# First input tiles given out by two DMA queues in one-tile pieces, first weight heads split on VectorE, seven warm-up matmuls for nine

## The chip, the cores and the metric

The kernel runs on one core of one Trainium2 chip. The metric is the time of one execution in microseconds; three runs of the kernel before and one profiled execution are at hand. TensorE is PE in the profile, VectorE DVE, ScalarE ACT, GpSimd POOL; SP is the engine that only issues DMAs, and ACT and POOL can issue them too.

## What is computed

One layer of a hybrid decoder over 512 tokens of width 1024, all in f32. Only the start matters here: the first of the projections, of which the change touches three output tiles.

```
h = rms_norm(x, norm_mix)            # x: (512, 1024)
z = h @ w_in
... z_mq ... = split(z)              # z_mq: the queries of the memory cross-attention
```

After it come the other mixers, the output projection, a gated MLP with a short convolution, and a last norm.

## The kernel before

x lies transposed in eight tiles of 128 channels by 512 tokens (`xs["T"][k]`, m in the profile's names, k = 0 to 7). The first three query tiles (u = 0 to 2) are made by `start`: for each k and each u, a weight tile of 128x128 times x tile k, summed over k in three PSUM banks. For precision every f32 operand is split in two parts of the type f32r, a rounded one (hi) and the rest (lo), and three matmuls stand for one: hi x hi, hi x lo, lo x hi. So a k has 9 matmuls, and `start` has 72. RMSNorm's gain is put on x in the split of x (`x_split`: ACT makes hi at L371, DVE makes lo at L372); the row scale comes later.

`split` makes a weight's parts: ACT copies to hi (L97), DVE subtracts to lo (L98). In `start` the raw weights of unit u come in pieces of two k (128x256, 128 KB), between the x tiles (256 KB each), all on the SP queue. The gain column needed by `x_split` is in `prm`, whose first eight columns are a DMA of their own (L200), the first on the SP queue. The rest of `prm` is the seventh DMA there (L426).

Ahead of that, PE multiplies a tile of zeros (`warm`) NWARM = 9 times (L211) and ACT loads its function table with an Exp of one column (L208). The order on each engine is set by a scheduler from the order of the code and its own estimate of times, so an edit here can also move instructions later on. After `start` come three more query tiles (`qu`), x's mean square (L219 to L228), the scale broadcast (L237, L238), the eight normalized tiles (`x_norm`, L392) and the keys and values of the memory.

Of the kernel before, what the change touches and what calls it, by code (L numbers as in the profile page):

```python
# [8 lines left out]
F32 = mybir.dt.float32  # L9
# [4 lines left out]
AF = mybir.ActivationFunctionType  # L14
ALU = mybir.AluOpType
# [3 lines left out]
P = 128  # L19
D = 1024  # L20
KD = D // P
# [19 lines left out]
BRANCHES = (2, 0, 1)  # L41
NRAW = 3
HT = S // 2
NWARM = 9


C_GMIX = 0
# [10 lines left out]
def trunk(ctx: ExitStack, tc: tile.TileContext, x, xT, mem, memT, par, wdecay, wch, wv, wg, wmk,  # L58
          wmv, wrg, wbr, wout, wup, wdown, wdown2, gffn, gfin, out):
    nc = tc.nc  # L60
# [11 lines left out]
    def nm(s):  # L72
        uid[0] += 1
        return f"{s}_{uid[0]}"
# [4 lines left out]
    def rslot(shape=(P, S)):  # L79
        return apool.tile(list(shape), F32R, tag="s", name=nm("r"))  # L80

    def mslot(dt=F32, shape=(P, S)):
        return hpool.tile(list(shape), dt, tag="m", name=nm("m"), bufs=8)

    def bank(shape=(P, S)):
        return psm.tile(list(shape), F32, tag="mm", name=nm("mm"))

    def sbank(shape=(P, S)):
        return pss.tile(list(shape), F32, tag="sm", name=nm("sm"))

    def stat(n, p=P):
        return small.tile([p, n], F32, tag=f"st{n}", name=nm("st"), bufs=12)


    def split(hi, lo, src, eng=None):

        nc.scalar.activation(hi, src, AF.Copy)  # L97
        return (eng or nc.vector).tensor_tensor(out=lo, in0=src, in1=hi.bitcast(F32), op=ALU.subtract)  # L98
# [98 lines left out]

    HB = D // 2
    prm = const.tile([P, NPAR], F32, name="prm")
    nc.sync.dma_start(prm[:, :KD], par[:, :KD])  # L200
    ident = const.tile([P, P], F32, name="ident")
    make_identity(nc, ident)
    ones = const.tile([P, P], F32, name="ones")
# [1 line left out]

    warm = const.tile([P, P], F32, name="warm")
    nc.vector.memset(warm, 0.0)
    nc.scalar.activation(stat(1), warm[:, 0:1], AF.Exp)  # L208
    ps = sbank((P, P))
    for _ in range(NWARM):  # L210
        nc.tensor.matmul(ps, lhsT=warm, rhs=warm, start=True, stop=True)  # L211

    def col(c, p=P):
        return prm[:p, c:c + 1]
# [151 lines left out]
    xs = {"T": [mslot() for _ in range(KD)], "r": []}  # L366

    def x_split(ks):
        for k in ks:
            r, g, src = (rslot(), rslot()), col(C_GMIX + k), xs["T"][k]  # L370
            nc.scalar.activation(r[0], src, AF.Copy, scale=g)  # L371
            nc.vector.scalar_tensor_tensor(out=r[1], in0=src, scalar=g, in1=r[0].bitcast(F32),  # L372
                                           op0=ALU.mult, op1=ALU.subtract)
            xs["r"].append(r)

    def x_squares(ks):
        for k in ks:
            xs["acc"] = add_square(xs.get("acc"), xs["T"][k])
# [19 lines left out]
    def queries(ps):  # L398
        r = (rslot(), rslot())
        if len(mq) % 3 == 1:  # L400
            for q, own, other in zip(r, (slice(0, 64), slice(64, P)), (slice(64, P), slice(0, 64))):
                nc.scalar.activation(q[own], ps[own], AF.Copy)
                nc.vector.tensor_tensor(out=q[other], in0=ps[own], in1=q[own].bitcast(F32), op=ALU.subtract)
        else:
            split(*r, ps)
        mq.append(r)

    def start():


        n = 3
        raw = [wpool.tile([P, D], F32, tag="raw", name=nm("raw"), bufs=NRAW) for _ in range(n)]
        whi, wlo = ([[wpool.tile([P, D], F32R, tag=t, name=nm(t))] for _ in range(2)] + [[rslot(), rslot()]]
                    for t in ("whi", "wlo"))

        def w(a, u, k, m=1):
            j, k = divmod(k, KD // len(a[u]))
            return a[u][j][:, k * P:(k + m) * P]

        for k in range(0, KD, 2):  # L420
            nc.sync.dma_start(xs["T"][k], xT[:, k, :])
            for u in range(n):
                nc.sync.dma_start(raw[u][:, k * P:(k + 2) * P], wch[u][:, k * P:(k + 2) * P])
            nc.sync.dma_start(xs["T"][k + 1], xT[:, k + 1, :])
            if k == 0:
                nc.sync.dma_start(prm[:, KD:], par[:, KD:])  # L426
        for k in range(0, KD, 2):
            x_split([k])
            for u in range(n):
                split(w(whi, u, k, 2), w(wlo, u, k, 2), raw[u][:, k * P:(k + 2) * P])  # L430
            x_split([k + 1])
        ps = [bank() for _ in range(n)]
        for k in range(KD):
            seq = [(whi, u, j) for j in range(2) for u in range(n)] + [(wlo, u, 0) for u in range(n)]
            for i, (a, u, j) in enumerate(seq):
                nc.tensor.matmul(ps[u], lhsT=w(a, u, k), rhs=xs["r"][k][j], start=k == 0 and i < n,  # L436
                                 stop=k == KD - 1 and i >= len(seq) - n)
        x_squares(range(4))
        for p in ps:
            queries(p)  # L440

    step(start)
    qu = [(wch[i], D, lambda w: queries(channel_major(w, KD, lambda k: xs["r"][k]))) for i in range(3, NM)]
    xn = [lambda k=k: x_norm(k) for k in range(KD)]
# [1073 lines left out]
```

## Time and profile before

| | |
|---|---|
| median of three runs | 923.41 us (923.1 to 926.32) |
| profiled execution, its own time | 924.37 us |
| profiled execution, span from first to last instruction | 922.6 us |
| mean granted TensorE clock | 0.997 |
| PE busy | 912.0 us, 99% of the span |

The span is the stretch of the recorded instructions; the execution's own time holds 1.77 us more around it. PE's busy time is the time in which a matmul was under way, waiting inside a matmul's record included.

### The profile page before, as it was taken

The numbers are of one execution on the slowest core, as the hardware profiler recorded it, in microseconds if no ns is written. First come the engines' busy times: TensorE is split into PE (matmuls) and PEld (weight loads), VectorE is DVE, ScalarE is ACT, GpSimd is POOL, SyncE is SP. The second block draws the span as 40 slices with busy tenths as digits, with TensorE's granted clock in tenths as the row PEclk, the third lists the DMA queues.
The fourth block names the chain that finished last, engine by engine and source line by source line (L and its number), as shares of the span: only waits on it lengthen the run. The fifth ranks groups of instructions, "written<-read, shape, count | busy, mean of one in ns | idle before, by whom it ended". The sixth has DMA issues, their size and how long they took to land.

```text
span 922.6 us, 12732 instructions
## 1 busy us (share of the span) xinstructions
PE 912.0 (99%) x4606; PEld 784.1 (85%) x4606; DVE 657.2 (71%) x1168; ACT 524.1 (57%) x888; POOL 128.1 (14%) x168
## 2 busy tenths in 40 slices
PE   9999999999999999999999999999999999999997
PEld 7899888888889998888888898998988888888885
DVE  6997755665689568746766678767787757598765
ACT  7765655685865468474534446555555445445544
POOL 0010000000243430320000000222111130013102
PEclk9999999999999999999999999999999999999998
DMA  7446223213467884321157313675646785357622
GB/s 238 148 137 214 92 88 101 88 42 119 110 170 167 187 204 126 115 86 53 52 157 258 116 59 90 157 185 130 148 114 165 145 228 125 114 137 181 139 69 91
DMA packets 51183, 123.27 MB, mean 134 GB/s; under 512 B 6145, under 2 KB 14001, under 8 KB 51121
## 3 DMA queue, kind: packets, MB, share of 16 engines
q1 hardware_dynamic: 35648, 94.99, 31.6%
q0 software_dynamic: 15328, 27.21, 17.3%
q8 instruction: 36, 0.59, 0.3%
q10 hardware_dynamic: 144, 0.26, 0.1%
q14 instruction: 27, 0.21, 0.1%
HBM read 117.99 MB, written 3.67 MB: 132 GB/s over the span
## 4 chain that ended last, share of the span: by engine, by line
PE 87%; DMA 5%; DVE 3%; issue 2%; ACT 2%; POOL 0%; SPq 0%; DVEq 0%; POOLq 0%; ACTq 0%
PE mm L104 78%; DMA f<-in_wup 4%; PE sm L104 3%; DMA f<-in_wv 2%; PE mm L436 2%; DVE wlo L98 1%; DVE r L98 1%; ACT r L97 1%; PE sm L211 0%; PE sm L996 0%; PE sm L983 0%; PE sm L1010 0%; DVE f L810 0%; PE sm L1147 0%; PE sm L601 0%
## 5 line engine op out<-in xcount | busy, mean ns | idle before, releaser
L97 ACT ACTIVATE whi<-raw 128x1024 fp32r<-128x1024 f32 (+3 forms) x142 | 135.5, 961 | 144.4 <-PE mm L104 113.1
L98 DVE TENSOR_TENSOR wlo<-raw,whi 128x1024 fp32r<-128x1024 f32 (+3 forms) x142 | 157.4, 1113 | 82.8 <-ACT whi L97 39.4
L104 PE MATMUL mm<-whi,r 128*128 128x512 f32 (+2 forms) x568 | 171.2, 372 | 0.0
L104 PEld LDWEIGHTS mm<-whi,r 128*128 128x128 f32 x568 | 105.5, 188 | 15.9 <-ACT r L97 0.3
L104 PE MATMUL mm<-hh,whi 128*128 128x512 f32 x288 | 113.4, 394 | 0.0
L104 PE MATMUL mm<-hl,whi 128*128 128x512 f32 x288 | 112.8, 392 | 0.0
L104 PE MATMUL mm<-wlo,r 128*128 128x512 f32 (+2 forms) x284 | 105.7, 372 | 0.5 <-DVE wlo L98 0.5
L104 PE MATMUL mm<-h2l,whi 128*128 128x512 f32 x264 | 102.8, 390 | 0.0
L104 PE MATMUL mm<-h2h,whi 128*128 128x512 f32 x264 | 102.7, 390 | 0.0
L98 DVE TENSOR_TENSOR r<-f,r 128x512 fp32r<-128x512 f32 (+3 forms) x144 | 79.7, 577 | 23.0 <-ACT r L97 22.7
L104 PE MATMUL mm<-r,whi 128*128 128x512 f32 (+1 forms) x432 | 94.2, 367 | 0.0
L97 ACT ACTIVATE r<-f 128x512 fp32r<-128x512 f32 (+3 forms) x144 | 70.1, 535 | 34.1 <-DMA f<-in_wup 29.2
L98 DVE TENSOR_TENSOR wlo<-f,whi 128x512 fp32r<-128x512 f32 (+2 forms) x90 | 53.8, 631 | 47.5 <-ACT whi L97 40.6
L104 PEld LDWEIGHTS mm<-r,whi 128*128 128x128 f32 x432 | 75.2, 189 | 13.1
L97 ACT ACTIVATE whi<-f 128x512 fp32r<-128x512 f32 (+2 forms) x90 | 48.2, 579 | 62.5 <-PE mm L104 48.8
L104 PE MATMUL mm<-hh,wlo 128*128 128x512 f32 x288 | 71.4, 390 | 0.0
L104 PE MATMUL mm<-r,r 128*128 128x512 f32 (+2 forms) x336 | 65.7, 346 | 0.3 <-ACT r L97 0.3
L104 PE MATMUL mm<-h2h,wlo 128*128 128x512 f32 x264 | 65.2, 389 | 0.0
L104 PEld LDWEIGHTS mm<-hh,wlo 128*128 128x128 f32 x288 | 54.0, 188 | 11.2
L104 PEld LDWEIGHTS mm<-hh,whi 128*128 128x128 f32 x288 | 54.1, 188 | 10.8
L104 PEld LDWEIGHTS mm<-hl,whi 128*128 128x128 f32 x288 | 54.1, 188 | 10.7
L104 PEld LDWEIGHTS mm<-r,r 128*128 128x128 f32 (+1 forms) x336 | 53.3, 186 | 9.6 <-ACT r L97 0.5
(261 smaller groups left out, 1545.2 us busy)
## 6 DMA issues: line engine op xcount, KB each, us to landing
raw<-in_wch SPq DMA_DIRECT2D x39, 512.0 KB, 3.3
raw<-in_wup SPq DMA_DIRECT2D x36, 512.0 KB, 4.0
f<-in_wdown POOLq DMA_DIRECT2D x40, 256.0 KB, 7.0
raw<-in_wbr SPq DMA_DIRECT2D x24, 384.0 KB, 3.1
raw<-in_wdown SPq DMA_DIRECT2D x14, 512.0 KB, 3.8
f<-in_wup SPq DMA_DIRECT2D x24, 256.0 KB, 6.9
f<-in_wup POOLq DMA_DIRECT2D x24, 256.0 KB, 6.4
f<-in_wdown SPq DMA_DIRECT2D x20, 256.0 KB, 4.7
```

The source lines that it names most:

```text
L97: nc.scalar.activation(hi, src, AF.Copy)
L98: return (eng or nc.vector).tensor_tensor(out=lo, in0=src, in1=hi.bitcast(F32), op=ALU.subtract)
L104: nc.tensor.matmul(ps, lhsT=l, rhs=r, start=first and i == 0, stop=last and i == len(seq) - 1, skip_group_check=more)
L436: nc.tensor.matmul(ps[u], lhsT=w(a, u, k), rhs=xs["r"][k][j], start=k == 0 and i < n, stop=k == KD - 1 and i >= len(seq) - n)
```

## The change

The first k gets pieces of its own. Its three weight heads (columns 0 to 127 of each unit) and the small `prm` piece are issued on the ACT queue; x tiles 0 and 1 and the second heads (columns 128 to 255) on the SP queue; the large `prm` piece on the POOL queue. The table load with its Exp now stands behind ACT's four DMA issues. The first heads' hi and lo are both made on DVE (a copy, then a subtraction); x tile 0 is split after them, and the second heads after the hi part of x tile 0. Pieces from k = 2 on are as before. Two warm-up matmuls are left out.

```diff
-NWARM = 9
+NWARM = 7
...
-    nc.sync.dma_start(prm[:, :KD], par[:, :KD])
+    nc.scalar.dma_start(prm[:, :KD], par[:, :KD])
...
-    nc.scalar.activation(stat(1), warm[:, 0:1], AF.Exp)
...
-            nc.scalar.activation(r[0], src, AF.Copy, scale=g)
+            xs["head"] = nc.scalar.activation(r[0], src, AF.Copy, scale=g)
...
-        for k in range(0, KD, 2):
+
+        nc.sync.dma_start(xs["T"][0], xT[:, 0, :])
+        for u in range(n):
+            nc.scalar.dma_start(raw[u][:, :P], wch[u][:, :P])
+        nc.scalar.activation(stat(1), warm[:, 0:1], AF.Exp)
+        nc.sync.dma_start(xs["T"][1], xT[:, 1, :])
+        for u in range(n):
+            nc.sync.dma_start(raw[u][:, P:2 * P], wch[u][:, P:2 * P])
+        nc.gpsimd.dma_start(prm[:, KD:], par[:, KD:])
+        for k in range(2, KD, 2):
             nc.sync.dma_start(xs["T"][k], xT[:, k, :])
...
-            if k == 0:
-                nc.sync.dma_start(prm[:, KD:], par[:, KD:])
-        for k in range(0, KD, 2):
+        for u in range(n):
+            nc.vector.tensor_copy(w(whi, u, 0), raw[u][:, :P])
+            nc.vector.tensor_tensor(out=w(wlo, u, 0), in0=raw[u][:, :P], in1=w(whi, u, 0).bitcast(F32), op=ALU.subtract)
+        x_split([0])
+        with tc.issue_after(xs["head"].ins):
+            x_split([1])
+        with tc.issue_after(xs["head"].ins):
+            for u in range(n):
+                split(w(whi, u, 1), w(wlo, u, 1), raw[u][:, P:2 * P])
+        for k in range(2, KD, 2):
             x_split([k])
```

On ACT, at the program's start, this stood before (m is an x tile, raw a weight piece, whi and the r made from raw are weight hi parts):

```order
L208 ACT_TABLE_LOAD
L208 ACTIVATE st_87<-warm 128x1
L371 ACTIVATE r_158<-m_101,prm 128x512
L97 ACTIVATE whi_129<-raw_126 128x256
L97 ACTIVATE whi_130<-raw_127 128x256
L97 ACTIVATE r_131<-raw_128 128x256
L371 ACTIVATE r_168<-m_102,prm 128x512
```

and this stands there now, with every line number behind the edit moved on by up to 15:

```order
L200 DMA prm<-in_par 128x8
L422 DMA raw_122<-in_wch 128x128
L422 DMA raw_123<-in_wch 128x128
L422 DMA raw_124<-in_wch 128x128
L423 ACT_TABLE_LOAD
L423 ACTIVATE st_137<-warm 128x1
L370 ACTIVATE r_165<-m_97,prm 128x512
L370 ACTIVATE r_169<-m_98,prm 128x512
L97 ACTIVATE whi_125<-raw_122 128x128
L97 ACTIVATE whi_126<-raw_123 128x128
L97 ACTIVATE r_127<-raw_124 128x128
```

Four DMA issues came ahead of the table load, and the three weight copies between x tile 0 and x tile 1 went away.

On DVE, right behind the zeroing of `warm`, this stood before:

```order
L372 SCALAR_TENSOR_TENSOR r_159<-m_101,prm,r_158 128x512
L98 TENSOR_TENSOR wlo_133<-raw_126,whi_129 128x256
L98 TENSOR_TENSOR wlo_134<-raw_127,whi_130 128x256
L98 TENSOR_TENSOR r_135<-raw_128,r_131 128x256
L372 SCALAR_TENSOR_TENSOR r_169<-m_102,prm,r_168 128x512
```

and this stands there now:

```order
L434 CAST whi_125<-raw_122 128x128
L435 TENSOR_TENSOR wlo_129<-raw_122,whi_125 128x128
L434 CAST whi_126<-raw_123 128x128
L435 TENSOR_TENSOR wlo_130<-raw_123,whi_126 128x128
L434 CAST r_127<-raw_124 128x128
L435 TENSOR_TENSOR r_131<-raw_124,r_127 128x128
L371 SCALAR_TENSOR_TENSOR r_166<-m_97,prm,r_165 128x512
L371 SCALAR_TENSOR_TENSOR r_170<-m_98,prm,r_169 128x512
```

Six instructions of 128x128 came ahead of the lo part of x tile 0 (r_166 now, r_159 before).

On PE the first k's nine matmuls stood like this before (r_158 and r_159 are hi and lo of x tile 0):

```order
L211 MATMUL sm_89<-warm 128x128 x9
L436 MATMUL mm_214<-r_158,whi_129 128x512
L436 MATMUL mm_215<-r_158,whi_130 128x512
L436 MATMUL mm_214<-r_159,whi_129 128x512
L436 MATMUL mm_215<-r_159,whi_130 128x512
L436 MATMUL mm_216<-r_158,r_131 128x512
L436 MATMUL mm_216<-r_159,r_131 128x512
L436 MATMUL mm_214<-r_158,wlo_133 128x512
```

and now (r_165 and r_166 are hi and lo of x tile 0):

```order
L210 MATMUL sm_87<-warm 128x128 x7
L451 MATMUL mm_221<-r_165,whi_125 128x512
L451 MATMUL mm_222<-r_165,whi_126 128x512
L451 MATMUL mm_223<-r_165,r_127 128x512
L451 MATMUL mm_221<-r_166,whi_125 128x512
L451 MATMUL mm_222<-r_166,whi_126 128x512
L451 MATMUL mm_223<-r_166,r_127 128x512
L451 MATMUL mm_221<-r_165,wlo_129 128x512
```

The third unit's hi matmul moved up to third place, ahead of the three with x's lo part. Behind `start` the same instructions stand on PE, DVE and ACT, some of them a few rows earlier or later, up to about the 465th row of PE's list; from there on the lists agree. SP issues two DMAs fewer, those of `prm`, ahead of x tile 2.

## Rows read from the trace of the kernel before

**Rows 1.** Page: the span; PE's busy time, share and instructions.
```profile
span 922.6 us, 12732 instructions
PE 912.0 (99%) x4606; PEld 784.1 (85%) x4606; DVE 657.2 (71%) x1168; ACT 524.1 (57%) x888; POOL 128.1 (14%) x168
```

**Rows 2.** Timeline of PE, 0 to 26 us: start, us, operation, idle before.
```profile
1.13 4.21 PE L211 MATMUL sm<-warm 128*128 128x128 f32 x18 [1.13 <-DVE warm L207]
5.26 1.90 PE L436 MATMUL mm<-r,whi 128*128 128x512 f32 x4
7.00 0.63 PE L436 MATMUL mm<-r,r 128*128 128x512 f32 x2
...
8.16 0.63 PE L436 MATMUL mm<-r,whi 128*128 128x512 f32 x2
...
22.46 3.79 PE L104 MATMUL mm<-r,whi 128*128 128x512 f32 x16
```

**Rows 3.** Timeline of PE, 24 to 140 us: the rows with idle time before.
```profile
67.85 0.44 PE L104 MATMUL mm<-wlo,r 128*128 128x384 f32 x1 [0.49 <-DVE wlo L98]
105.15 0.55 PE L620 MATMUL sm<-ident,f 128*128 128x128 f32 x3 [0.26 <-ACT f L607]
```

**Rows 4.** Timeline of ACT, 0 to 9 us.
```profile
0.81 1.28 ACT L208 ACT_TABLE_LOAD   x1 [0.81 <-PEq L1507]
2.10 0.20 ACT L208 ACTIVATE st<-warm 128x1 f32<-128x1 f32 x1
4.18 0.72 ACT L371 ACTIVATE r<-m,prm 128x512 fp32r<-128x512 f32 x1 [1.87 <-DMA m<-in_xT]
4.80 0.40 ACT L97 ACTIVATE whi<-raw 128x256 fp32r<-128x256 f32 x1
...
7.07 0.73 ACT L371 ACTIVATE r<-m,prm 128x512 fp32r<-128x512 f32 x1 [0.30 <-DMA m<-in_xT]
```

**Rows 5.** Chain of work, 0 to 130 us: start, us, what.
```profile
5.34 17.28 PE mm L436 x72
...
41.69 0.22 PE sm L238 x2
```

**Rows 6.** Timeline of PE's weight loads around 6.3 us.
```profile
6.15 0.34 PEld L436 LDWEIGHTS mm<-r,whi 128*128 128x128 f32 x1
6.54 0.19 PEld L436 LDWEIGHTS mm<-r,whi 128*128 128x128 f32 x1
```

**Rows 7.** Timeline of SP's DMA issues, 0 to 9 us.
```profile
0.81 0.39 SPq L200 DMA_DIRECT2D prm<-in_par  x1
1.26 0.43 SPq L421 DMA_DIRECT2D m<-in_xT  x1
1.74 1.37 SPq L423 DMA_DIRECT2D raw<-in_wch  x3
```

**Rows 8.** Timeline near the end: the one DMA issue on ACT's queue.
```profile
918.96 0.37 ACTq L1390 DMA_DIRECT2D out<-f  x1
```

**Rows 9.** Landing of x 0, weight pieces 0 and 2, x 1 (us from issue).
```profile
m<-in_xT SPq DMA_DIRECT2D x1, 256.0 KB, 2.8
raw<-in_wch SPq DMA_DIRECT2D x1, 128.0 KB, 2.7
raw<-in_wch SPq DMA_DIRECT2D x1, 128.0 KB, 3.6
m<-in_xT SPq DMA_DIRECT2D x1, 256.0 KB, 3.9
```

**Rows 10.** Line L237, DVE on 128x128: duration in ns, min/median/max.
```profile
L237 DVE TENSOR_SCALAR dg<-ident,st x6: 278/282/334, 40.9 to 53.3; 128x128 f32<-128x128 f32 x6
```

**Rows 11.** Timeline of DVE, 0 to 9 us.
```profile
4.93 0.75 DVE L372 SCALAR_TENSOR_TENSOR r<-m,prm,r 128x512 fp32r<-128x512 f32 x1 [3.86 <-ACT r L371]
5.60 0.79 DVE L98 TENSOR_TENSOR wlo<-raw,whi 128x256 fp32r<-128x256 f32 x2
```

**Rows 12.** Windows, DVE alone: stretch, us, busy (instructions), clock, DMA, GB/s.
```profile
50.00:54.00 4.00, 4.00 (x11) 1.00 0.28 94
```

## The prediction

> **What bounds the kernel now.** I read the page first. PE is busy 912.0 of 922.6 us [rows 1], so only what keeps PE from its next matmul can pay, and the whole idle time is 10.6 us. Then PE's timeline [rows 2]: the warm-ups run from 1.13 to 5.34, the first matmul of `start` begins at 5.26, the second k at 8.16, and `start` is done at 22.46, when the next unit follows without a gap. From 8.16 to 22.46 lie 63 matmuls, k = 1 to 7, so one takes 14.30 / 63 = 0.227 us and PE never waits in that stretch. The first k's nine matmuls would need 9 x 0.227 = 2.04 us and take 8.16 - 5.26 = 2.90. This is the only place that the change can shorten directly, together with the 5.26 us ahead of it. From 24 to 140 us PE stands idle in two places only, 0.49 and 0.26 us [rows 3]. So an earlier end of `start` moves all later work on PE, as long as those two waits don't grow.
>
> Why the first k is slow: its hi matmul waited for the weight's hi part, which ACT made from 4.80 to 5.20, after x tile 0's hi part from 4.18 to 4.90 [rows 4]; ACT itself had waited 1.87 us for x tile 0. And PE runs at its lower level there. A warm-up pass of 128 columns takes 4.21 / 18 = 0.234 us, while the like pass at L238 takes 0.22 / 2 = 0.11 [rows 2, 5]: 1.2 against 2.4 GHz. The weight load at 6.15 still takes 0.34 us, the one at 6.54 takes 0.19 [rows 6], so the clock rises between them, near 6.4, after PE has worked without a long pause since 1.13. (The column of the granted clock shows 1.00 throughout, so durations are my guide.) A matmul of 512 columns costs about 2 x 0.227 = 0.45 us before that moment.
>
> **The change part by part.**
>
> *ACT's queue and x tile 0.* SP's issues start 0.45 to 0.48 us apart [rows 7]; the only issue on ACT's queue takes 0.37 [rows 8]. Four of them ahead of the table load take 4 x 0.37 = 1.5 to 4 x 0.46 = 1.84 us; I take the upper value, since those of SP are at the same place in the program. ACT gets to the table load at 0.81 + 1.84 = 2.65, ends it at 3.93 and the Exp at 4.13 [rows 4]. x tile 0 is now issued at 0.81 and not at 1.26, and with 2.8 us to landing [rows 9] it is there at about 3.6. So its split begins at about 4.15 (lower bound 3.85, by the shorter issues), against 4.18: this part gains nothing, since ACT takes the place of the DMA as the last to come. Hi of x tile 0 is ready at 4.15 + 0.72 = 4.87.
>
> The table load stands right before the Exp [rows 4]: 1.28 us, and the Exp starts 0.01 us later. The Trainium skill (ScalarE: Activation LUTs, What ACT_TABLE_LOAD costs) adds a drain of about 1.38 us to the load of 1.28, some 2.66 together. By the page the split of x would begin at about 5.5, by the row at 4.15: the trace agrees with the load's length and shows no drain behind it, and what stands behind four DMA issues no row shows.
>
> *The weight heads on DVE.* They are issued at about 1.27, 1.73 and 2.19, each 64 KB. Of the 128 KB pieces the first took 2.7 us to land, the third 3.6 [rows 9], behind x tile 0 in one queue. I take 2.7 for all, as half the bytes: 4.0, 4.45, 4.9; upper bound for the third, with 3.6, 5.8. A DVE instruction of 128x128 takes 0.28 us [rows 10], so a head's copy and subtraction take 0.57. The first hi part is there at 4.3, before x's hi part. So the first matmul begins at 4.87 + 0.03 = 4.9, against 5.26. The last pair ends at 4.9 + 0.57 = 5.5 (upper bound 6.4). DVE's lo part of x tile 0 is queued behind it, where before it was DVE's first work at 4.93 [rows 11]: now 5.5 to 6.25 (upper bound 7.15).
>
> *PE.* Three hi matmuls at 0.45 each run 4.9, 5.35, 5.8, to 6.25; the third head's hi part (5.2) is in time. The next six, which need x's lo part, can go at 6.3. If the clock rises near 6.4 as before, they take 6 x 0.227 = 1.36 us and the first is a little slower: the second k begins at 7.7, against 8.16. **Gain: 0.45 us.** With the upper bound of the landings the lo part is there at 7.15 and the second k begins at 8.55, a loss of 0.4; with the lower bound of ACT's issues the three hi matmuls are over by 6.0, DVE still sets 6.25, and the gain stays at about 0.5.
>
> *The warm-ups.* Seven end at 1.13 + 14 x 0.234 = 4.41, so two fewer never hold up the first matmul; PE then idles 0.5 us. That costs nothing unless the clock answers to it (first rival).
>
> *The later tiles.* x tile 1, issued at 1.27, lands with at most 3.9 us [rows 9] at 5.2 (before: 7.07 [rows 4]); ACT makes its hi part until 5.9, then three heads of 128x128; DVE makes its lo part until 7.0 and three heads at 0.28 until 7.85, needed at 7.7 + 6 x 0.227 = 9.1. No wait. SP has two `prm` issues fewer ahead of x tile 2, so that is no later than before, and from there on PE had the data in time without a gap. The large `prm` piece goes through POOL, free by then; it is read first by a small ACT instruction at about 12 us. Nothing.
>
> *The reordered instructions and the wait at 67.85.* PE's place is given to it by DVE there [rows 3], and DVE is busy without a pause in 50 to 54 us [rows 12]. If DVE doesn't come earlier by as much, part of the 0.45 goes into that wait. DVE's work is released by PE's own results from further back (the mean square and broadcast matmuls), so most should move along; I take 0.05 off.
>
> Sum: 0.45 - 0.05 = 0.4. The profiled execution's own 924.37 becomes 923.97; it lies 0.96 above the median of 923.41, and against that median I forecast **923.0 us**, 0.04% less. A measurement of this kernel can tell about 0.5% (4.6 us) from no change, more than `start`'s whole lead of 5.26 us is likely to give.
>
> **Rivals.**
>
> *The clock rises later* (slower). PE has less work before 6.4: warm-ups until 4.41, an idle half microsecond, three matmuls. The Trainium skill (TensorE: Matmul & The Clock Gate, What's actually happening) says that the low clock is the default and that activity releases it, which speaks against taking warm-ups out; the rows above agree that the first 5 us run at the low level. No row gives a later moment for the rise; as a bound I let it come with the third k of the old order, at 10.2: until then PE does (10.2 - 4.9) / 0.45 = 11.8 matmuls, where before 9 + (10.2 - 8.16) / 0.227 = 18 were done. The loss is 6.2 x 0.227 = 1.4 us, so **924.8**. It decides from a rise later than about 7.3: each 0.45 us more at the low level costs one matmul's 0.227, so 0.9 us of it cost the whole gain. For it speaks the gap; against it that PE also had a gap before, inside the 1.90 us of the first four matmuls.
>
> *ACT or the heads are late* (a new wait). A pause on ACT as long as the table load itself, 1.28, would make x's hi part ready at 6.15 and begin the second k at about 6.3 + 2.04 = 8.35, a loss of 0.2; the upper landing bound gave a loss of 0.4. With 0.3 this is **923.7**. For it speaks that four issues are put ahead of the table load; against it that the row shows the load followed by the Exp at once. The drain in the Trainium skill (ScalarE: Activation LUTs, What ACT_TABLE_LOAD costs) would be such a pause.
>
> *The gain is eaten at 67.85.* The wait grows from 0.49 to 0.9 and **923.4** stays.
>
> *More than forecast.* The clock rises when it did or earlier, the lo part is ready at 6.0, and one of the two later waits vanishes by the new order: 0.45 + 0.25 + 0.49 = 1.2, so **922.2**.
>
> **How the numbers follow.** Forecast 0.40, late clock 0.20, late ACT or heads 0.15, eaten 0.13, more 0.10, something unseen 0.02. The range reaches from the "more" case to the late clock, with the spread of the shown executions around their median (0.3 below, 1 above) taken in half: 921.9 to 925.0. No case comes near 4.6 us: faster 0.01, same 0.97, slower 0.02.
>
> **What would show it.** Right: ACT's split of x tile 0 at 4.0 to 4.2, held by its own queue and not by the DMA; the first matmul at 4.8 to 5.0; the second k at 7.6 to 7.8; the next unit at about 22.0 and not 22.46; the wait at 67.85 still about 0.5. Wrong: weight loads of 0.3 us after 6.6, DVE's lo part of x tile 0 after 6.5, or the Exp more than 1.3 us after the table load's start.

## The result and the profile after

The changed kernel is slower: 928.62 us (median of 22 runs, 925.66 to 932.34) against 925.54 for the kernel before (22 runs beside them, 922.14 to 927.31). The ratio is 1.0037, 95% interval 1.0027 to 1.0046, so some 3.1 us. That is less than the 0.5% named in the prediction, but it is a loss, where a gain of 0.4 was forecast, and the time lies above the range. Of the 5.6 us between 923.0 and 928.62, 2.1 are the kernel before's own: the median of its 22 runs is 925.54, where the three runs at hand had 923.41. The rest is the loss of 3.1 and the gain of 0.4 that did not come.

The profiled execution took 929.63 us. Its page, for [rows 1]:

```profile
span 927.7 us, 12737 instructions
PE 913.4 (98%) x4602; PEld 783.5 (84%) x4602; DVE 657.6 (71%) x1174; ACT 523.1 (56%) x888; POOL 128.3 (14%) x169
```

PE is busy 1.4 us longer with two warm-ups fewer, and idle 14.3 us where it was 10.6. The start of its timeline, for [rows 2] (the last row is cut off by its window):

```profile
1.13 3.19 PE L210 MATMUL sm<-warm 128*128 128x128 f32 x14 [1.13 <-DVE warm L207]
5.66 0.89 PE L451 MATMUL mm<-r,whi 128*128 128x512 f32 x2 [1.34 <-DVE whi L434]
6.80 0.49 PE L451 MATMUL mm<-r,r 128*128 128x512 f32 x1 [0.25 <-DVE r L434]
7.79 1.22 PE L451 MATMUL mm<-r,whi 128*128 128x512 f32 x2 [0.49 <-DVE r L371]
...
10.51 0.79 PE L451 MATMUL mm<-r,whi 128*128 128x512 f32 x2
...
25.00 2.20 PE L104 MATMUL mm<-r,whi 128*128 128x512 f32 x9
```

The first matmul comes at 5.66 (before: 5.26, forecast: 4.9), the second k at 10.51 (8.16, 7.7), the next unit at 25.00 (22.46, 22.0): 2.54 us late. Three waits stand where before there was no pause over 0.2 us: for the first weight head, for the third, and for the lo part of x tile 0. Who was late is seen on DVE, for [rows 11], and on ACT, for [rows 4]:

```profile
5.29 0.23 DVE L434 CAST whi<-raw 128x128 fp32r<-128x128 f32 x1 [4.22 <-DMA raw<-in_wch]
...
6.52 0.23 DVE L434 CAST r<-raw 128x128 fp32r<-128x128 f32 x1 [0.20 <-DMA raw<-in_wch]
6.78 0.29 DVE L435 TENSOR_TENSOR r<-raw,r 128x128 fp32r<-128x128 f32 x1
6.99 1.41 DVE L371 SCALAR_TENSOR_TENSOR r<-m,prm,r 128x512 fp32r<-128x512 f32 x2
```

```profile
1.24 1.42 ACTq L422 DMA_DIRECT2D raw<-in_wch  x3
2.69 1.28 ACT L423 ACT_TABLE_LOAD   x1 [2.69 <-issue]
3.99 0.20 ACT L423 ACTIVATE st<-warm 128x1 f32<-128x1 f32 x1
4.21 1.55 ACT L370 ACTIVATE r<-m,prm 128x512 fp32r<-128x512 f32 x2
```

ACT did what was forecast to within 0.06 us. DVE waited for the heads. They land later than the 2.7 us taken for them (median us from issue, at the line's end; the small `prm` piece took 1.8 us before, as the first of SP's queue):

```profile
raw<-in_wch ACTq DMA_DIRECT2D x3, 64.0 KB, 4.0
prm<-in_par ACTq DMA_DIRECT2D x1, 4.0 KB, 3.4
```

And the clock: windows of PE alone (stretch, us, busy and instructions, granted clock, DMA share, GB/s).

```profile
6.00:7.00 1.00, 0.75 (x3) 1.00 0.91 237
7.00:8.00 1.00, 0.51 (x2) 0.72 0.77 249
8.00:9.00 1.00, 1.00 (x3) 0.50 0.90 228
...
10.00:11.00 1.00, 1.00 (x4) 0.58 0.89 224
11.00:12.00 1.00, 1.00 (x6) 1.00 1.02 348
```

0.50 is the 1.2 GHz level, granted while PE did its six matmuls behind the waits. They take 0.45 us each, 10.51 - 7.79 = 2.72 us in all, where 1.36 was forecast. The column reads 1.00 from the start, for the slow warm-ups too, so a duration has to tell of the level ahead of 7 us. Such a weight load took 0.34 us at the low level before the change [rows 6]; here the first one takes 0.19, so the high level was there already, and was taken back:

```profile
5.63 0.19 PEld L451 LDWEIGHTS mm<-r,whi 128*128 128x128 f32 x1 [1.51 <-ACT r L370]
```

SP's queue is late too, for [rows 7]; the row behind it is from the list of SP's waits (total, times, longest):

```profile
1.72 2.81 SPq L426 DMA_DIRECT2D raw<-in_wch  x3
4.57 0.43 SPq L429 DMA_DIRECT2D m<-in_xT  x1
...
12.64 0.43 SPq L432 DMA_DIRECT2D m<-in_xT  x1
```

```profile
SPq L426 <- DMA prm<-in_par: 1.6, 1, 1.6
```

The third second-head waits 1.6 us for the small `prm` piece of the other queue to land (in the trace both DMAs tell of their landing by the same semaphore), and x tile 2 is issued at 4.57, before at 4.10. The last x tile is issued at 12.64; before, it was

```profile
11.39 0.43 SPq L424 DMA_DIRECT2D m<-in_xT  x1
```

Behind `start` the waits of [rows 3] stay as they were, one 0.49 and now 0.51, the other 0.26 and now 0.22:

```profile
69.70 0.44 PE L104 MATMUL mm<-wlo,r 128*128 128x384 f32 x1 [0.51 <-DVE wlo L98]
107.50 0.55 PE L635 MATMUL sm<-ident,f 128*128 128x128 f32 x3 [0.22 <-ACT f L622]
```

A weight split on ACT that PE releases shows the lag a little later, first of the kernel before and then of the changed one: 111.43 - 108.62 = 2.81 us. I call it the mark at 108.62 below.

```profile
108.62 1.06 ACT L97 ACTIVATE whi<-raw 128x1024 fp32r<-128x1024 f32 x1 [2.85 <-PE mm L104]
```

```profile
111.43 1.06 ACT L97 ACTIVATE whi<-raw 128x1024 fp32r<-128x1024 f32 x1 [3.31 <-PE mm L104]
```

The spans differ by 5.1 us, but 2.3 of such a difference is not the change's: a second profile of the unchanged kernel (e8_before_again) has a span of 924.9 with its mark at 109.01, only 0.39 later. The first profile of before is a short one. So the loss to be explained is the median's 3.1, and the first 110 us hold about as much. Behind them the lag stays as it is for a long time: the same six matmuls, before and now, lie 302.58 - 299.77 = 2.81 us apart.

```profile
299.77 1.52 PE L104 MATMUL mm<-r,wlo 128*128 128x512 f32 x6
```

```profile
302.58 1.52 PE L104 MATMUL mm<-r,wlo 128*128 128x512 f32 x6
```

### The profile page after: what moved, and what is told of

It reads as the page before. It is cut to its first block, busy times and chain, and to the rows that moved or that the text cites. A ratio compares the mean times of both kernels' runs of the same rounds, so it can differ in the third digit from the quotient of the medians.

```text
span 927.7 us, 12737 instructions
## 1 busy us (share of the span) xinstructions
PE 913.4 (98%) x4602; PEld 783.5 (84%) x4602; DVE 657.6 (71%) x1174; ACT 523.1 (56%) x888; POOL 128.3 (14%) x169
## 4 chain that ended last, share of the span: by engine, by line
PE 86%; DMA 6%; DVE 5%; ACT 2%; issue 1%; POOL 0%; SPq 0%; DVEq 0%; POOLq 0%; ACTq 0%
PE mm L104 77%; PE sm L104 4%; DMA f<-in_wv 2%; PE mm L451 2%; DMA f<-in_wup 2%; DVE wlo L98 1%; DVE r L98 1%; DVE f L1186 1%; DMA f<-in_wdown 1%; ACT whi L97 0%; PE sm L1011 0%; DMA raw<-in_wmv 0%; PE sm L998 0%; PE sm L616 0%; PE sm L1025 0%
## 5 line engine op out<-in xcount | busy, mean ns | idle before, releaser
L98 DVE TENSOR_TENSOR wlo<-raw,whi 128x1024 fp32r<-128x1024 f32 (+4 forms) x142 | 157.1, 1111 | 85.8 <-ACT whi L97 49.4
L97 ACT ACTIVATE whi<-raw 128x1024 fp32r<-128x1024 f32 (+4 forms) x142 | 135.6, 959 | 145.1 <-PE mm L104 109.1
L104 PEld LDWEIGHTS mm<-hh,whi 128*128 128x128 f32 x288 | 54.1, 188 | 10.8
```

The source lines that it names most:

```text
L104: nc.tensor.matmul(ps, lhsT=l, rhs=r, start=first and i == 0, stop=last and i == len(seq) - 1, skip_group_check=more)
```

## The experiments

All but three kernels were timed beside the kernel before. For each: the next unit's start on PE (22.46 before), the end of the last addition that the mean-square matmul needs (30.41 + 0.69 = 31.10 before; start and duration of DVE's fourth addition of squares in that stretch), the mark at 108.62, and the ratio. The five kernels that undo the order of the instructions come behind the table.

| kernel | next unit | sum ready | mark | ratio, 95% interval |
|---|---|---|---|---|
| before, first profile | 22.46 | 31.10 | 108.62 | |
| before, second profile | 22.84 | 31.49 | 109.01 | one profile |
| before, 7 warm-ups | 23.80 | 32.44 | 109.97 | 1.0008 [0.9991, 1.0025] |
| before, `prm` off SP | 23.41 | 32.05 | 110.78 | 1.0045 [1.0025, 1.0064] |
| before, small `prm` on ACT | 22.83 | 31.47 | 109.01 | 0.9997 [0.9986, 1.0009] |
| change | 25.00 | 34.40 | 111.43 | 1.0037 [1.0027, 1.0046] |
| change, second profile | 24.07 | 34.78 | 113.49 | one profile |
| change, 12 warm-ups | 23.37 | 33.63 | 110.45 | 1.0034 [1.0017, 1.0051] |
| change, 9 warm-ups | 23.59 | 34.69 | 113.45 | 1.0051 [1.0034, 1.0068] |
| change, heads on SP | 24.62 | 33.27 | 112.27 | 1.0045 [1.0027, 1.0063] |
| change, heads split on ACT | 24.37 | 33.01 | 112.91 | 1.0048 [1.003, 1.0066] |
| change, large `prm` on SP | 24.04 | 32.95 | 112.73 | 1.0063 [1.0045, 1.0081] |
| change, x tile 1 later | 23.55 | 33.16 | 109.92 | one profile |
| the same, timed | 24.84 | 33.81 | 111.44 | 1.0038 [1.0023, 1.0053] |
| the same, 9 warm-ups | 23.12 | 33.98 | 111.09 | 1.0025 [1.001, 1.004] |

One profile stands behind each row, and executions differ: the change's own start, in four profiles (two of them of kernels whose edit comes behind it), began its next unit at 23.44, 24.07, 24.98 and 25.00. A difference of less than that between two rows of the changed kernel shows little. The lag at the mark goes with the ratio, though: among the timed kernels it is 0.4 and 1.35 us where the ratio cannot be told from 1, and 1.8 us or more (to 4.8 in this table) where it is 1.0025 or above.

**Warm-ups.** First the clock: more warm-ups in the change, fewer in the kernel before.

```diff
-NWARM = 7
+NWARM = 12
```

> The changed kernel with twelve warm-up matmuls in place of seven; they end at about 1.13 + 24 x 0.23 = 6.7 us. Theory A, that the clock fell in the pause between the warm-ups and the late first matmuls: the six matmuls behind the wait for x tile 0's lo part take 0.23 us each and not 0.45, the second k begins at about 9.2 (changed kernel: 10.51), the next unit at about 23.6 (25.00), and the time is some 1.4 us below the changed kernel's, so about 1.002 of the kernel before. Theory B, that the late weight heads are the whole loss and the clock none: the first matmul is only pushed from 5.66 to 6.75, the second k begins at 10.5 or later and the time is that of the changed kernel or above, 1.004.

With 12 the clock rises at about 4.7 and stays. Its first k on PE:

```profile
5.53 0.82 PE L451 MATMUL mm<-r,whi 128*128 128x512 f32 x2
6.59 0.49 PE L451 MATMUL mm<-r,r 128*128 128x512 f32 x1 [0.23 <-DVE r L434]
7.58 0.73 PE L451 MATMUL mm<-r,whi 128*128 128x512 f32 x2 [0.49 <-DVE r L371]
...
9.07 0.62 PE L451 MATMUL mm<-r,whi 128*128 128x512 f32 x2
```

The waits are the same, but the six matmuls take 9.07 - 7.58 = 1.49 us and not 2.72. Against the change's first profile the clock is worth 1.2 us. Yet the whole was hardly faster: a new wait of 0.72 us stood before the mean-square matmul, and 1.0034 cannot be told from 1.0037.

> The kernel before with seven warm-up matmuls in place of nine, its loads and splits untouched. Theory A: the pause of 0.85 us between 4.41 and 5.26, and the waits among the first four matmuls, hold the clock down or make it fall, so the second k begins later than 8.16, up to 9.5, and the time rises by up to 1.4 us (1.000 to 1.0015). Theory B: the warm-ups themselves matter nothing, the second k stays at 8.2 and the next unit at 22.5 (1.000).

In the kernel before, nine turned into seven cost 1.34 us at the next unit (the second k at 9.50), again with a later clock, and none of it grew or was lost up to the mark. In time that was 1.0008, unclear as to sign.

> The changed kernel with its two warm-ups given back: nine, to 5.34. Clock theory: the pause before the first matmul at 5.5 to 5.7 is short, so the clock is high sometime between 4 and 8 and does not fall again in most executions; the second k begins between 9.1 (clock never in the way) and 10.5, and the time lies between the one with twelve warm-ups and the changed kernel's, 1.002 to 1.003. If the warm-ups do not matter: second k at 10.5 as in the changed kernel, 1.0037.

Nine warm-ups in the change brought the next unit to 23.59, 1.4 us earlier than with seven in the first profile and 0.5 earlier than in the second, and ended at 1.0051. This is where the gain went, the mean-square matmul, and the clock in the windows behind it:

```profile
34.84 1.02 PE L227 MATMUL sm<-ones,f 128*128 128x1 f32 x8 [1.57 <-DVE f L220]
```

```profile
36.00:37.00 1.00, 1.00 (x4) 0.57 0.48 74
37.00:38.00 1.00, 1.00 (x4) 0.50 0.83 307
38.00:39.00 1.00, 1.00 (x4) 0.50 0.38 152
39.00:40.00 1.00, 1.00 (x5) 0.72 0.68 193
```

PE comes earlier, waits 1.57 us for the sum of squares, and then works for some 3 us at the low level. By these rows that takes 0.43 + 0.50 + 0.50 + 0.28 = 1.7 us of clock, as much again as the wait (an estimate: the missing shares of the four windows).

**Heads.** One edit puts the heads on SP's queue (`nc.sync` for `nc.scalar` at L422), one lets `split` make them on ACT and DVE, behind `x_split([0])`, as before.

> The changed kernel with the three weight heads issued on SP's queue, between x tile 0 and x tile 1, and only the small parameter piece on ACT's queue; pieces, DVE work and seven warm-ups stay. Theory C, that two queues side by side made the heads wait for both x tiles: in one queue the heads land behind x tile 0 alone, at about 4.1, 4.6 and 5.1 us (changed kernel: 5.24, 5.7, 6.4), the first matmul begins at about 4.9 and the lo part of x tile 0 is made from 5.7 (6.99); the second k begins at about 7.8 if the clock is high by then and 9 if not, and the time is 1.5 to 3 us below the changed kernel's. Theory D, that rows of 512 bytes are slow whatever the queue: the heads land no earlier than 5.2 and the time is the changed kernel's.

> The changed kernel with the first heads split as before, hi on ACT behind x tile 0's hi part and lo on DVE behind its lo part; loads and seven warm-ups stay. If the six DVE instructions ahead of x tile 0's lo part are a part of the loss: that lo part is made from about 5.0 and not 6.99, the six matmuls that waited for it go on right behind the third head, and the second k begins about 1 us earlier than 10.51, with a clock that falls less. If the loss is the landing of the heads alone: the first matmul at about 5.8, the third at 7.0, and the second k between 9 and 10.5, by the clock.

In one queue, behind x tile 0, the first head was split at 4.09 and not 5.29, but the second only at 5.19 and the third at 5.99: about as far apart as twice as large pieces are before. x's lo part came at 6.46, the clock fell as in the change, and the time did not improve (1.0045), with a wait of 1.60 us at 108.58 that stood at 0.26 before. With the heads split as before, x's lo part was made from 4.84, the first matmul began at 5.26 and the third head's hi part at 6.14, all as early as before; but the clock rose only at 10.5, and four waits of 0.24 to 0.73 us came between 33 and 61 us (1.0048). So neither the queue nor DVE's queue alone is the cause.

**x tile 1.** Issued behind the second heads, in one profile and then timed.

```diff
-        nc.sync.dma_start(xs["T"][1], xT[:, 1, :])
         for u in range(n):
             nc.sync.dma_start(raw[u][:, P:2 * P], wch[u][:, P:2 * P])
+        nc.sync.dma_start(xs["T"][1], xT[:, 1, :])
```

> The changed kernel with x tile 1 issued behind the three second weight heads on SP's queue. Theory C (the first heads on ACT's queue wait for the large x tiles of SP's queue, row by row): with one x tile less in front the first head lands at about 4.5 (changed kernel: 5.24), and DVE's first copy begins there. Theory D (rows of 512 bytes, or ACT's queue itself, are slow): the first copy stays at 5.2 or comes later.

> The change with x tile 1 issued behind the second heads, seven warm-ups, timed. In its one look the lag behind before was 1.1 us at the next unit and about 1.5 us later, without a wait at the mean square. If that repeats: 1 to 2 us above before, ratio 1.001 to 1.002. If the look was a lucky one: ratio 1.003 or more with a wait at the mean square.

DVE in the first of the two:

```profile
4.42 0.23 DVE L434 CAST whi<-raw 128x128 fp32r<-128x128 f32 x1 [3.35 <-DMA raw<-in_wch]
...
5.84 0.23 DVE L434 CAST whi<-raw 128x128 fp32r<-128x128 f32 x1 [0.87 <-DMA raw<-in_wch]
```

Without x tile 1 beside it the first head comes 0.87 us earlier, the second does not. That repeats: the first copy begins at 4.41 to 4.48 in four more profiles with this edit, and at 5.05 to 5.37 in seven with x tile 1 issued early and nothing else moved ahead of it. In time the first profile was a lucky one: there the clock rose at 5.1, in the timed run's profile only at 10.8, and the ratio is 1.0038, as for the change.

**The `prm` pieces.** The kernel before with the small piece on ACT's queue and the large one on POOL's; the change with the large piece back on SP, behind the second heads; the kernel before with the small piece on ACT and the large one on SP with the third group.

> The kernel before with only its two parameter DMAs taken off SP's queue, the small one to ACT's queue ahead of the table load, the large one to POOL's; nine warm-ups, two-tile weight pieces and splits on ACT as before. If SP's issues set the first landings, x tile 0 and the three weight pieces come 0.45 us earlier: ACT's split of x tile 0 begins at about 3.75 (4.18 before), the second k at about 7.7 with a clock that is high by then and at most 8.2 otherwise, and the time falls by 0 to 0.5 us (0.9995 to 1.000). If instead the small piece lands late because it shares the DMA engines with x tile 0 (3.4 us in the changed kernel against 1.8), the split begins at 4.2 and nothing moves (1.000).

> The changed kernel with the large parameter piece back on SP's queue, behind the second weight heads. Theory F, that the piece on POOL's queue shares the DMA engines with the first heads: the three first heads land 0.3 to 0.5 us earlier, copies from 4.9, x tile 0's lo part from 6.5, and x tile 2 later by the piece's own issue. If it does not matter, the copies stay at 5.2.

> The kernel before with the small parameter piece on ACT's queue ahead of the table load and the large one put back on SP's queue to the third group, nine warm-ups, two-tile pieces, splits on ACT. Nothing shares the engines with the first pieces but the small one: x tile 0's split begins at 3.9 (4.18 to 4.32 before), the weight pieces' at 4.6, 5.2 and 6.0, the second k at about 7.8 (8.16 to 8.56) by the clock, and the time falls by 0.3 to 0.5 us, 0.9995, at most 1.000. If the pieces land no earlier although they are issued earlier, as they did with both parameter pieces off SP's queue (5.7 and 7.15), it is the same or slower.

The first is slower than before, 1.0045: with the large piece on a queue of its own beside the weight pieces, the second and third of those were later (hi parts at 4.55, 5.73 and 7.17 where they had begun at 4.80, 5.51 and 6.34). Its profiled execution shows only 2.16 us at the mark, and was a short one of runs from 925.55 to 932.57. In the change, with the large piece off POOL the heads did land earlier, as was expected if it shares in their delay (copies from 4.93, x's lo part from 6.33), and the time was no better (1.0063). The last is the best version of the study and no different from the kernel before, 0.9997. The first and the last differ in the place of the large piece alone (and in what the scheduler made of it): that place is worth the whole of 1.0045 against 0.9997. Nothing that was tried beats the kernel before.

**The order behind `start`.** The two kernels were each profiled once more, to see what differs from execution to execution.

> The kernel before, unchanged, profiled once more. If the clock's rise comes at another moment in each execution: weight loads turn from 0.33 to 0.19 us somewhere between 4 and 8 us and not just at 6.4, never fall back, and the second k begins between 7.8 and 8.6; the next unit between 22.1 and 22.9. If the moment is fixed by the kernel: at 6.4 again, 8.16 and 22.46.

> The changed kernel, unchanged, profiled once more. Clock theory: the level seen by the first k depends on when in the execution the clock turns, which differs from one execution to the next; the weight heads' copies again begin at 5.1 to 5.4, x tile 0's lo part at 6.8 to 7.1, and the second k somewhere between 9.1 (clock high by then) and 10.8 (low). If the loss were fixed by the program: 10.51 and 25.00 again.

The second profile of the change began its next unit earlier than the first, at 24.07, and was at 113.49 at the mark, 2 us later than the first. Again the mean-square matmul:

```profile
34.93 1.02 PE L227 MATMUL sm<-ones,f 128*128 128x1 f32 x8 [1.19 <-DVE f L220]
```

with the clock at 0.50 from 37 to 39 us. So the two profiles lost at different places. In the first, 25.00 - 22.46 = 2.54 us of the 2.81 at the mark stood at the next unit already. In the second it was 24.07 - 22.46 = 1.61 of 4.87, and the wait of 1.19 and the low clock behind it make most of the rest. Why the sum is late is seen on ACT, first in the kernel before, then in the change's first profile, then in its second (the squares are L219 and L218):

```profile
25.40 1.05 ACT L97 ACTIVATE whi<-raw 128x1024 fp32r<-128x1024 f32 x1
26.34 2.18 ACT L219 ACTIVATE f<-m 128x512 f32<-128x512 f32 x4
```

```profile
26.13 1.06 ACT L97 ACTIVATE whi<-raw 128x1024 fp32r<-128x1024 f32 x1 [0.31 <-DVE r L98]
...
28.37 1.06 ACT L97 ACTIVATE whi<-raw 128x1024 fp32r<-128x1024 f32 x1
29.33 2.17 ACT L218 ACTIVATE f<-m 128x512 f32<-128x512 f32 x4
```

```profile
26.57 1.06 ACT L97 ACTIVATE whi<-raw 128x1024 fp32r<-128x1024 f32 x1 [1.68 <-DMA raw<-in_wch]
```

In the change, and in the versions of the table that only have more warm-ups or x tile 1 later, the scheduler put two things ahead of the squares: the third unit's weight split moved ahead of two copies of `start`'s queries, where it can wait for its DMA (1.68 us), and a fourth split, of `wmk`, stands before the squares instead of behind them (1.06). So the sum is ready at 33.2 to 34.8 there. The matmul that needs it stood at 31.76 before. As long as the sum comes then, PE can't be there with less than 33.2 - 31.76 = 1.4 to 34.8 - 31.76 = 3.0 us of lag, whatever the start gains.

This order is not needed for the loss, however. In three versions of the table ACT has the list of before up to the squares, by the scheduler's own choice: heads on SP, heads split on ACT, large `prm` on SP. Their sum is late about as PE is late (with the heads split on ACT 33.01 - 31.10 = 1.91, next unit 24.37 - 22.46 = 1.91), and their ratios are 1.0045 to 1.0063 all the same.

Then the order was undone by hand. In the first such kernel the fourth split is held behind the squares, with nine warm-ups.

```diff
+            xs["n"] = xs.get("n", 0) + 1
+            if xs["n"] == 4:
+                with tc.issue_after(xs["sq"].ins):
+                    split(hi, lo, raw)
```

> The changed kernel with nine warm-ups and with the first key weight's split held behind the squares of x tiles 4 to 7, as the order of the kernel before has it. Theory E, that the new order behind the first units makes PE wait for the mean square (0.72 and 1.57 us with twelve and nine warm-ups, none before): the wait at the mean-square matmul is under 0.3, the clock does not fall near 36 us, the lag behind the kernel before stays at about 1.1 us through to 300 us, and the time is 2 to 4 us below that with nine warm-ups alone (1.0051), at 1.001 to 1.003. If the order is not the cause, the wait and the time stay as they were.

The remedy failed, 1.0081 [1.0067, 1.0095]. The squares came at 28.40, still behind 1.98 us of waiting for the third unit's weights, and with this edit the mean-square matmul itself moved six places up on PE: it waited 1.58 us at 33.30. So it was held too, by emitting `x_rstd` one unit later and behind the second unit's sixteenth matmul, with the mended start and with the change's own.

> The change with x tile 1 issued behind the second heads, nine warm-ups, the split of the first wmk unit held behind the squares and the mean-square matmul held behind 16 or more matmuls of the second unit. If the loss is the start (late heads, late lo part, clock) plus the new order at the mean square, both are mended here: next unit at 23.0 to 23.6, no wait over 0.2 us at the mean square, no fall of the clock at 36 us, total within 1.2 us of before (ratio 1.000 to 1.0015). Rival, the order behind start costs nothing: the total equals that of e14_x1late_warm9. Rival, something later in the program costs the 3 us: ratio 1.003 or more as in the change.

> The change with x tile 1 issued behind the second heads and nine warm-ups; the order behind start stays the new one. If the order matters: next unit at 23.0 to 23.6, but then PE reaches the mean square earlier than its last sum and waits there 0.3 to 1.2 us, with a fall of the clock behind a wait of 1 us or more; total 1 to 4 us above before (ratio 1.001 to 1.004). Rival, start alone sets the loss: total at most 1 us above before.

> The change with its own start (seven warm-ups, x tile 1 early), but with the order of before at the squares: wmk split behind the squares, mean square behind 16 or more matmuls of the second unit. If the order carries a part of the loss: start's lag of 1.6 to 2.5 us stays, no wait at the mean square, total 1.6 to 2.6 us above before, ratio 1.0017 to 1.003. Rival, the order costs nothing: ratio 1.0037 as in the change.

With the start mended alone (nine warm-ups, x tile 1 later) the next unit began at 23.12, 1.9 us earlier than in the change, and the ratio is 1.0025, as expected. The wait at the mean square was 1.32 us, a little more than expected, and the clock did not fall behind it. With the order mended that wait is gone in both kernels, and the ratios are 1.0045 [1.0027, 1.0064] (start mended too) and 1.0038 [1.0019, 1.0057]. Both are above what was expected if the order mattered; the second is its rival's 1.0037. The waits came back further on, 2.08 us at 109.56 in the first, and in the second

```profile
45.05 0.49 PE L242 MATMUL sm<-dg,ones 128*128 128x128 f32 x2 [0.35 <-DVE dg L241]
...
107.69 0.55 PE L643 MATMUL sm<-ident,f 128*128 128x128 f32 x3 [1.17 <-ACT f L630]
```

In the first the clock was also low in the first k again (second k at 10.23) although it had nine warm-ups, and it fell to 0.50 once more behind the wait of 2.08 us, from 111 to 113 us. Last, the third split was held behind the queries too, so that ACT's list up to the squares is that of before.

```diff
+            if xs["n"] in (3, 4):
+                with tc.issue_after(xs["qa" if xs["n"] == 3 else "sq"].ins):
```

> As e13 (x tile 1 behind the second heads, the wmk split behind the squares, mean square later), with twelve warm-ups and with the split of the third unit's weights held behind the queries of start too, so that ACT's list from there to the squares is that of before. If the start's clock and the new order on ACT carry the loss: next unit at 23.0 to 23.4, no wait on ACT or PE of before's list grown, the wait at 105 to 110 us at most 0.4, total at most 1 us above before (ratio 0.9995 to 1.001). Rival, the input stream itself, 0.5 to 1.2 us later on DVE and ACT from 14 us on, sets the loss whatever the order: a wait of 0.5 us or more appears again between 26 and 110 us and the ratio is 1.0025 or more.

> As e16 (the change's own start, seven warm-ups), with the third unit's split held behind the queries of start too. If the order carries a part: only the start's lag of 1 to 2.5 us stays, no grown wait behind it, ratio 1.001 to 1.0027. Rival, the late input stream sets the loss whatever the order: the lag grows again between 26 and 110 us, ratio 1.0035 or more.

The ratios are 1.0032 [1.0011, 1.0052] and 1.0062 [1.0042, 1.0081]. The rival's condition came true in both: waits again, in the first kernel

```profile
43.48 0.49 PE L242 MATMUL sm<-dg,ones 128*128 128x128 f32 x2 [0.88 <-DVE dg L241]
59.18 2.18 PE L104 MATMUL mm<-r,whi 128*128 128x256 f32 x16 [0.66 <-DVE f L521]
```

and ACT there, with the order of before and a next unit only 1.04 us late, still waited for the input:

```profile
22.70 1.06 ACT L97 ACTIVATE whi<-raw 128x1024 fp32r<-128x1024 f32 x1 [1.65 <-DMA raw<-in_wch]
```

The waits at 43.48 and 59.18 can't be put down to the input alone, since the mean-square matmul stands seven matmuls later in these kernels than before the change, and the broadcast behind it moved along.

## Why the prediction was wrong

**The landing of the heads: the step that failed first.** "I take 2.7 for all, as half the bytes" was wrong in its size. They took 4.0 us and more, above the upper bound of 3.6 too, so DVE began at 5.29 where 4.0 was taken. The rows used were those of pieces in one queue, one behind the other; here six pieces of half the size, two x tiles and `prm` run together. That x tile 1 beside them delays the first head is shown (5.29 to 4.42 without it, 4.09 in one queue); that halving a piece doesn't halve the distance between landings is shown by the heads in one queue. The sum had a slip beside it: three pairs of 0.57 one behind the other from 4.0 on end at 5.7 and not at 5.5, so some 0.2 us of the gain does not follow from its own numbers.

**x's lo part.** The mechanism was named, "queued behind" the last pair, at 5.5 with an upper bound of 7.15: it was 6.99, past the 6.5 that the prediction gave as a sign of being wrong. PE's six matmuls began at 7.79 and not 6.3. Of the term "Gain: 0.45 us" nothing is left: at the full clock the second k would have come at 7.79 + 1.36 = 9.15, a loss of 1.0.

**The clock.** The step "If the clock rises near 6.4 as before" failed, and the first rival came true, by a way that it did not have: in this profile the high level was there before 6.4 and up to 7 us, was taken back between 7 and 8, behind PE's waits, and came again only after 10. It cost 1.36 us here (2.72 - 1.36), where the rival had 1.4; 12 warm-ups gave 1.2 back. That leaving two warm-ups out costs nothing by itself was not borne out either: in the profile of the kernel before with seven, the second k came at 9.50, though the time (1.0008) does not tell. But the level isn't fixed by the program: the same start had its second k at 9.16, 9.78, 10.40 and 10.51 in four executions, and with nine warm-ups at 8.82 to 10.23. The Trainium skill (TensorE: Matmul & The Clock Gate, What's actually happening) has activity releasing the clock; the first weight load behind the warm-ups agrees (0.19 us), and the windows show that the clock can be taken back within the first 8 us, behind a stretch of waits.

**ACT's queue.** Right to 0.06 us, in part by luck: the split needs the small `prm` piece too, whose landing the prediction left out, and that came at 0.81 + 3.4 = 4.2, so a quicker ACT would have gained nothing either. (The lower bound of 3.85 is 3.8 by its own terms; nothing hangs on it.) The Trainium skill (ScalarE: Activation LUTs, What ACT_TABLE_LOAD costs) adds a drain to the load; behind four DMA issues as well the trace shows none (Exp at 3.99, the split of x at 4.21).

**x tile 2, "no later than before".** Wrong: 4.57 against 4.10, because SP waited for the small `prm` piece. SP's stream stayed behind, and the first weight split behind `start` came at 20.02, before at 19.26.

**The large `prm` piece, "Nothing".** This term was put at nothing, and it is not: in the kernel before, with the small piece on ACT's queue, the large one on POOL's queue goes with 1.0045 [1.0025, 1.0064] and on SP's with 0.9997 [0.9986, 1.0009]. What it is worth inside the change is not settled, since there its way back to SP gave 1.0063.

**The reordered instructions, "I take 0.05 off".** The prediction watched the wait at 67.85, which kept its size. What it did not look at was the slack at the mean-square matmul: 31.76 - 31.10 = 0.66 us before, with the squares one split earlier on ACT. The rows of the change's order that moved "a few rows" used it up. That is why a mended start gave so little in this order: 9 or 12 warm-ups moved the next unit by 1.4 and 1.6 us against the change's first profile (0.5 and 0.7 against the second) and the time by nothing that can be told.

**The base and the range.** The spread that the range takes in, "0.3 below, 1 above", leaves out the third run at hand, 926.32, which lies 2.9 above the median; and taken in half, as it says, the range would be 922.05 to 925.3. Neither would have held 928.62.

**What stays open.** The lag of the change's two profiles is found: nearly all in the start in the first, a smaller part there and most of it at the mean square in the second. The start, the late input and the new order all take part, and where one was mended, waits at other places took over. How much of the 3.1 us each is worth is not settled. ACT's order up to the squares alone is not the cause: five kernels with the list of before there, three by the scheduler and two by hand, came out at 1.0032 to 1.0063. But the mean-square matmul moved on PE in all five (by one to seven places), and none mended the input without leaving out the heads. Only kernels without the heads and with the order of before gave the time of before (seven warm-ups, or the small `prm` piece on ACT's queue with the large one later on SP's). Why executions of any version differ by 1 to 2 us between 500 and 720 us was not looked into.

## What to carry to other kernels

Pieces that are cut smaller and given to a second queue need not be there sooner while the first queue is busy (here 4.0 us for 64 KB, where the first 128 KB had taken 2.7): take their landing from transfers that ran beside others, and look at what is queued behind the instruction that waits for them. Ahead of an edit to a start that a scheduler orders, look up the slack of the next few places where the bound engine meets another one (here 0.66 us at the mean square), since a gain ahead of it is worth no more than that slack lets through. Where the clock in the start differs from one execution to the next, one profile doesn't give the price of an edit there.

## What was not expected of the hardware

A DMA of 4 KB took 1.8 us to land as the first of its queue and 3.4 us beside a second queue with 256 KB tiles. The granted clock went down to 0.50, the 1.2 GHz level, for some 3 us behind waits of PE of 1.19, 1.57 and 1.58 us near 34 us and of 2.08 us near 109, in the middle of dense work, and not behind waits of 0.72 and 1.32 us at the first place (12 warm-ups; x tile 1 later with nine) or of 1.17 us at the second.
